# Down tile in two banks, dt by feature tile, and one chunk step's outputs behind a convolution's evacuation

## Chip, cores and metric

One core of a Trainium2 chip runs the whole kernel in one launch. The metric is the device time of that core in microseconds (us); the median of several runs is given. The engines are TensorE (PE, matmuls, with its weight loads shown as PEld), VectorE (DVE), ScalarE (ACT), GpSimd (POOL) and SyncE (SP), on whose queue the transfers (DMA) of this case are issued. Each engine works through its own instructions in order and waits on semaphores for the others.

## The reference, cut to what matters

One layer of a hybrid decoder: a half-step SwiGLU block, a mixer, a second half-step SwiGLU block, all with RMS norms, on 512 prompt tokens and 8 single-token samples (520 columns), width 1024, in float32.

```python
h = x
h = h + 0.5 * _swiglu(_rms_norm(h, ffn1_norm), w_gate1, w_up1, w_down1)   # FFN width 2816
m, p, c, s = _hybrid_mixer(_rms_norm(h, mix_norm), ...)
h = h + m
h = h + 0.5 * _swiglu(_rms_norm(h, ffn2_norm), w_gate2, w_up2, w_down2)
return _rms_norm(h, final_norm), ...

# the mixer
proj = h @ w_in                                  # u_pool | z | xbc | dt
pool_out = _pool_mix(u_pool, ...)                # window means of 2, 4, 8, 16 tokens, then a matmul per group
xbc = silu(causal_conv4(xbc));  dt = softplus(dt_raw + dt_bias)
# Mamba-2 SSD, per chunk of 128 tokens and group g of 8 heads (two groups):
Acs   = cumsum(dt * A)                           # within the chunk
y_diag = (C B^T * exp(Acs_l - Acs_s) * dt) x     # inside the chunk
y_off  = C h_prev * exp(Acs)                     # from the state of the chunk before
h_next = exp(Acs_last) * h_prev + B^T (exp(Acs_last - Acs) * dt * x)
y = rms_norm_per_group((y_diag + y_off + d_skip * x) * silu(z)) * ssd_norm
return cat(pool_out, y) @ w_out
```

## The kernel before, in words

Activations lie with the feature on the partition: `h` is 8 tiles of 128 x 520, and 520 columns are worked on in two `HALVES` of 260. A float32 product is made of three fp32r matmuls (`mm3`, lines 117, 120, 121): weights and activations are split in a high and a low part (`whi` by an ACT cast, line 107, `wlo` by a DVE subtraction, line 108; `xh` and `xl` likewise, lines 138 and 139).

The first SwiGLU block takes its 22 hidden tiles in chunks of 8, 8 and 6. At the end of a chunk, `down` makes the 8 output tiles `dn`, d = 0 to 7, each in a PSUM tile of two banks, one for each half (tag "BE", two such tiles; tag "A" is two tiles of one bank). One DVE instruction on 128 x 520 (`td`, line 369) scales a tile out of PSUM, and two adds (line 376) bring it into `h`. In the last chunk (`after` is set) each half then goes straight to the mixer's norm: `xh`, `xl`, a square on ACT (line 149) and a sum `acc` on DVE (line 150).

The mixer has a PSUM pool of 8 single banks, handed out in turn. It begins with the step size `dt`: 32 short matmuls (lines 639 to 642) into the two banks dt0 and dt1, one half after the other. Then come the input projections, convolutions and pooling, and the SSD work. The order of stages is written out by hand in `CONV_PLAN` and `GATE_PLAN`; letters name the stage: "x7" is the projection and convolution of x tile 7, "p3" the fourth pooling group, "c" and "m" its centring and mixing, "z" a z projection, "Aj" and "Bj" the two parts of chunk step j. Within and between stages a scheduler sets the order of instructions on each engine when the kernel is built; it weighs program order, dependences and its own cost model.

Chunk step j has chunk c = j % 4 and group g = j // 4, and its tiles carry both as two digits: step 1 is "10", step 2 "20", step 3 "30", step 4 "01". Part A (`ssd_a`): `pb` (a transpose and the scores), `px` (four transposes of X); a transfer `ab` (line 873) that spreads the cumulative sums of 8 heads over all partitions; `we` (line 877), 128 x 8 on POOL, then its exp; for c > 0 `E` and `cd`, exps of `ab` on ACT (lines 883, 885); the differences `ab` minus a per-token column, four by ACT (line 888) and four by DVE (line 890), and their exps (892, 893); `xdt` (line 895), DVE, which reads `px`; `xw` on POOL (line 898); `G`, the decay times the scores, in place in `ab` (line 899). Part B (`ssd_b`): matmuls `yo` (908), `pst` (911) and `yd` (914); the state `hst` (POOL 920, DVE 921); `E` times yo plus yd (924, 925); and four DVE instructions that add d_skip * X and write the output in X (line 928, "the outputs").

A projection's two banks are evacuated by `evac`, three DVE instructions (lines 622 to 624: half 0, the prompt part of half 1, the 8 samples) into `U` for a convolution or `PU` for a pooling group. Convolutions go on in `A` (ACT 708, DVE 710) and a SiLU into X (ACT 712, 713); pooling runs in doubling steps `PW` on POOL (line 742), then DVE (753) and casts. The order of DVE around the change, at 473 to 483 us of the profiled execution, was: hst10, the outputs of step 1, two ab30, U7's half 0, two ab30 and four ab01, U7's half 1 and samples, PW3, xdt30, E20, wlo_inz2. A wait for the convolution of x tile 7 is one for U7.

## Time and profile before

| what | value |
|---|---|
| median of 3 runs | 993.21 us (992.85 to 993.3) |
| the profiled execution | 992.8 us, its span 991.0 us |
| granted TensorE clock | 0.997 |
| busy: PE, DVE, ACT, POOL | 969.8, 800.0, 552.8, 87.4 us |
| chain that ended last | PE 90%, DVE 5%, POOL, DMA, ACT and issue 1% each |

The span runs from the first to the last instruction. Rows of instructions read: start in us, duration in us, engine, line, operation, output and inputs, shape, count, and in brackets the idle time before it with what ended it. Rows of waits read: engine, what waited, what it waited for, then total us, number of times, longest. A row of the windows gives the stretch, its length, the busy time and number of instructions of PE, PEld, DVE, ACT and POOL, then the granted clock, the DMA share and GB/s. One matmul is shown for 0.28 us though the next starts 0.12 us after it: they are pipelined.

### The profile page before, as it was taken

The page shows a single profiled execution, that of the slowest core. Times are in us where ns is not written, and L with a number is a line of the kernel's source. Part 1 is how long each engine was busy: PE and PEld are TensorE (multiplying, and loading weights), DVE is VectorE, ACT ScalarE, POOL GpSimd, SP SyncE. Part 2 cuts the span into 40 slices and gives each one's busy share as a digit, 9 for nine tenths or more (in the row PEclk, how much of TensorE's full clock was granted, in tenths as well). Part 3 has the DMA queues.
Part 4 walks back from the last instruction along what each step waited for, and adds up shares of the span by engine and source line. Part 5 has one row for each costly group of instructions (what it writes and reads, how often), then busy time and mean ns, then how long its engine had stood idle before and what let it go on. Part 6 is the DMA issues. An engine that isn't in the chain of part 4 may idle for free.

```text
span 991.0 us, 19414 instructions
## 1 busy us (share of the span) xinstructions
PE 969.8 (98%) x7852; PEld 951.0 (96%) x7852; DVE 800.0 (81%) x1295; ACT 552.8 (56%) x1011; POOL 87.4 (9%) x157
## 2 busy tenths in 40 slices
PE   7999999999999999999999999999999999999996
PEld 6899999999999999999899999899999999999995
DVE  7999656997569688788978997999967899668876
ACT  7566414664136455685668574666643566534653
POOL 0000000000000000156522000100013000120000
PEclk9999999999999999999999999999999999999998
DMA  6332322323222232262335232323246423363212
GB/s 188 121 128 95 120 86 86 128 86 129 85 86 81 91 126 85 82 206 100 124 114 186 81 125 86 113 98 128 100 117 198 162 88 127 120 181 119 96 65 87
DMA packets 42027, 114.48 MB, mean 116 GB/s; under 512 B 6408, under 2 KB 13512, under 8 KB 41936
## 3 DMA queue, kind: packets, MB, share of 16 engines
q1 hardware_dynamic: 38864, 103.78, 30.6%
q0 software_dynamic: 3072, 9.44, 3.7%
q8 instruction: 62, 1.02, 0.4%
q14 instruction: 29, 0.24, 0.1%
HBM read 105.86 MB, written 7.34 MB: 114 GB/s over the span
## 4 chain that ended last, share of the span: by engine, by line
PE 90%; DVE 5%; POOL 1%; DMA 1%; issue 1%; ACT 1%; SPq 0%; DVEq 0%; ACTq 0%
PE A L121 8%; PE A L117 8%; PE A L120 8%; PE dn L121 7%; PE dn L117 7%; PE dn L120 7%; PE BE L117 6%; PE BE L121 6%; PE BE L120 6%; PE wo L117 2%; PE wo L121 2%; PE wo L120 2%; PE P L234 2%; PE inz L117 2%; PE inz L121 2%; PE inz L120 2%
## 5 line engine op out<-in xcount | busy, mean ns | idle before, releaser
L117 PE MATMUL dn<-g,whi_1d 128*128 128x260 f32 x352 | 99.3, 283 | 0.2 <-DVE td L369 0.2
L120 PE MATMUL dn<-g,whi_1d 128*128 128x260 f32 x352 | 99.5, 283 | 0.0
L121 PE MATMUL dn<-g,wlo_1d 128*128 128x260 f32 x352 | 99.4, 283 | 0.0
L369 DVE SCALAR_TENSOR_TENSOR td<-dn,r_f 128x520 f32<-128x520 f32 x40 | 27.8, 698 | 72.7 <-PE dn L121 72.7
L121 PE MATMUL dn<-g,wlo_2d 128*128 128x260 f32 x256 | 72.5, 283 | 0.8 <-DVE wlo_2d L108 0.8
L117 PE MATMUL dn<-g,whi_2d 128*128 128x260 f32 x256 | 72.3, 282 | 0.0
L120 PE MATMUL dn<-g,whi_2d 128*128 128x260 f32 x256 | 72.3, 282 | 0.0
L117 PEld LDWEIGHTS dn<-g,whi_1d 128*128 128x128 f32 x352 | 66.1, 188 | 0.4 <-DVE td L369 0.4
L120 PEld LDWEIGHTS dn<-g,whi_1d 128*128 128x128 f32 x352 | 66.3, 188 | 0.0
L121 PEld LDWEIGHTS dn<-g,wlo_1d 128*128 128x128 f32 x352 | 66.2, 188 | 0.0
L299 ACT COPY ac<-A 128x260 f32<-128x260 f32 x123 | 45.6, 374 | 28.9 <-PE A L121 28.0
L107 ACT CAST whi_1d<-raw_1d 128x1024 fp32r<-128x1024 f32 (+1 forms) x24 | 23.5, 981 | 67.0 <-PE dn L120 54.2
L262 DVE TENSOR_TENSOR s<-raw 128x1024 f32<-128x1024 f32 x41 | 49.9, 1218 | 5.6 <-DMA raw<-in_w2gu 5.6
L234 PE MATMUL P<-xg_f,raw 128*128 128x260 f32 x192 | 45.4, 392 | 6.4 <-ACT sq_f L157 5.5
L121 PEld LDWEIGHTS dn<-g,wlo_2d 128*128 128x128 f32 x256 | 48.2, 188 | 1.0 <-DVE wlo_2d L108 1.0
L234 PEld LDWEIGHTS P<-xg_f,raw 128*128 128x128 f32 x192 | 36.9, 196 | 12.2 <-ACT sq_f L157 5.4
L117 PEld LDWEIGHTS dn<-g,whi_2d 128*128 128x128 f32 x256 | 48.3, 189 | 0.0
L120 PEld LDWEIGHTS dn<-g,whi_2d 128*128 128x128 f32 x256 | 48.2, 188 | 0.0
L117 PE MATMUL wo<-catg,whi_wo 128*128 128x260 f32 x128 | 37.2, 290 | 0.0
L117 PE MATMUL inz<-xh_mx,whi_inz 128*128 128x260 f32 x128 | 36.8, 287 | 0.1
L117 PE MATMUL inx<-xh_mx,whi_inx 128*128 128x260 f32 x128 | 36.4, 284 | 0.0
L121 PE MATMUL wo<-catg,wlo_wo 128*128 128x260 f32 x128 | 36.2, 283 | 0.0
(1341 smaller groups left out, 3936.7 us busy)
## 6 DMA issues: line engine op xcount, KB each, us to landing
raw<-in_w2gu SPq DMA_DIRECT2D x44, 512.0 KB, 4.5
raw<-in_w1gu SPq DMA_DIRECT2D x42, 512.0 KB, 4.5
raw_1d<-in_w1d SPq DMA_DIRECT2D x16, 512.0 KB, 4.5
raw_2d<-in_w2d SPq DMA_DIRECT2D x16, 512.0 KB, 4.4
raw_wo<-in_w_out SPq DMA_DIRECT2D x12, 512.0 KB, 4.9
ab<-scr_acs SPq DMA_DIRECT2D x8, 512.0 KB, 4.9
h<-in_state_ssm SPq DMA_DIRECT2D x16, 256.0 KB, 3.7
raw_inz<-in_w_in SPq DMA_DIRECT2D x8, 512.0 KB, 3.8
```

The costliest lines, as they stand in the source:

```text
L107: nc.scalar.copy(h, src)
L117: first = nc.tensor.matmul(ps, whi, xhi, start=start, stop=False, **kw)
L120: nc.tensor.matmul(ps, whi, xlo, start=False, stop=False, **kw)
L121: nc.tensor.matmul(ps, wlo, xhi, start=False, stop=stop, **kw)
L234: nc.tensor.matmul(self.banks[f, u][b][:, :HB], ws(self.raw[f][:, u], j + 4 * q), xg[:, slot[q]], start=j == q == 0, stop=j == 3 and q == ...
L262: nc.vector.tensor_tensor(out=s1, in0=diag, in1=up0, op=ALU.add)
L299: nc.scalar.copy(keep, out[:, :HB])
L369: nc.vector.scalar_tensor_tensor(out=t, in0=banks[d][:, :, :HB], scalar=-0.5, in1=self.nx[3].rearrange("p (b t) -> p b t", b=2), op0=ALU.mult,
```

## The change

Four edits, of which the third has two sides:

1. In the first block's last chunk, down tile 7 goes into two single banks (tag "A") instead of one two-bank tile, and each half is evacuated by itself (`done_by_half`: a 128 x 260 scale, an add, then the norm's preparation), at high priority.
2. dt's matmuls run over the feature tiles outside and the halves inside.
3. `we` moves from POOL to DVE, and `xdt` stands ahead of it in the program; `E` and `cd` get three buffers instead of two.
4. The four outputs of chunk step 1 are not issued in "B1" but by a stage "Y1" after "x7", and the scheduler may place them only behind the last evacuation instruction of that convolution (`held["evac"]`).

```diff
-    "b0 b1 d0 ... x6 c2 p3 A2 B1 x7 "
+    "b0 b1 d0 ... x6 c2 p3 A2 B1 x7 Y1 "
...
-                    banks[d] = ps[0].tile([P, 2, 512], F32, tag="BE", bufs=2, name=f"dn{self.i}_{d}_{c}")
+                    if after is not None and d == KD - 1:
+                        banks[d] = [ps[0].tile([P, 512], F32, tag="A", bufs=2, name=f"dn{self.i}_{d}_{c}{b}")
+                                    for b in range(2)]
+                    else:
+                        t = ps[0].tile([P, 2, 512], F32, tag="BE", bufs=2, name=f"dn{self.i}_{d}_{c}")
+                        banks[d] = t[:, 0], t[:, 1], t
...
+            def done_by_half(d):
+                for b, hs in enumerate(HALVES):
+                    t = self.wx.tile([P, 2, HB], F32, tag="tg", bufs=2, name=f"td{self.i}_{d}_{c}{b}")[:, b]
+                    nc.vector.scalar_tensor_tensor(out=t, in0=banks[d][b][:, :HB], scalar=-0.5, in1=self.nx[3][:, hs],
+                                                   op0=ALU.mult, op1=ALU.mult)
+                    nc.vector.tensor_tensor(out=h[:, d, hs], in0=t, in1=h[:, d, hs], op=ALU.add)
+                    after(d, b, hs)
...
-                done(d)
+                if after is not None and d == KD - 1:
+                    with tc.high_priority():
+                        done_by_half(d)
+                else:
+                    done(d)
...
-        nc.vector.tensor_tensor(out=buf[:, soff : ...], in0=bs[1][:, nb:HB],
+        held["evac"] = nc.vector.tensor_tensor(out=buf[:, soff : ...], in0=bs[1][:, nb:HB],
...
-    for b, hs in enumerate(HALVES):
-        for k in range(KD):
+    for k in range(KD):
+        for b, hs in enumerate(HALVES):
...
+        xdt = mp.tile([P, 8, 64], F32, tag="xdt", bufs=2, name=f"xdt{c}{g}")
+        nc.vector.tensor_tensor(out=xdt, ...)            # moved up from behind the exps
         we = mp.tile([P, 8], F32, tag="we", bufs=2, name=f"we{c}{g}")
-        nc.gpsimd.tensor_tensor(out=we, in0=ab[:, :, CH - 1], in1=atc, op=ALU.subtract)
+        nc.vector.tensor_tensor(out=we, in0=ab[:, :, CH - 1], in1=atc, op=ALU.subtract)
...
-            E = mp.tile([P, 4, P], F32, tag="E", bufs=2, name=f"E{c}{g}")
+            E = mp.tile([P, 4, P], F32, tag="E", bufs=3, name=f"E{c}{g}")
-            cd = mp.tile([P, 8], F32, tag="cd", bufs=2, name=f"cd{c}{g}")
+            cd = mp.tile([P, 8], F32, tag="cd", bufs=3, name=f"cd{c}{g}")
...
+        def out():
+            for q in range(4):
+                nc.vector.scalar_tensor_tensor(out=X[:, 4 * g + q, cs], ...)
+        if (c, g) == ssd(1):
+            held["out"] = out
+        else:
+            out()
+
+    def ssd_out(_):
+        with tc.issue_after(held["evac"]):
+            held.pop("out")()
```

How the built program moves: PE's order stays but for dt and two places of a few matmuls. ACT runs E30 and cd30 ahead of the SiLU of A5, with two more table loads, and we30 and the exponentials of ab30 ahead of the cast whi_inz0. SP issues out_nps ahead of the first half of raw_inz4, and ab01 behind both. DVE's order around x tile 7 becomes: E10, hst10, we01, three ab01, U7's half 0, one ab01, U7's half 1 and samples, the outputs of step 1, PW3, wlo_inz2, xdt30, E20; we30 and the four ab30 stand between U6's half 0 and half 1. In the first block, wlo_inbc0 stands ahead of tile 6's adds, and the halves of tile 7 between the xl and acc of tile 6.

More of the change, by code (lines that the diff above doesn't have):

```diff
@@ L39 @@
 CONV_PLAN = (
-    "b0 b1 d0 b2 b3 x0 x1 v0 d1 x2 x3 d2 X0 p0 y0 c0 A0 p1 x4 m0 x5 B0 c1 p2 m1 A1 x6 c2 p3 A2 B1 x7 "
+    "b0 b1 d0 b2 b3 x0 x1 v0 d1 x2 x3 d2 X0 p0 y0 c0 A0 p1 x4 m0 x5 B0 c1 p2 m1 A1 x6 c2 p3 A2 B1 x7 Y1 "
     "c3 X1 m2 A3 B2 e0"
@@ L363, in part @@
                         g = self.g[lo + k]
-                        mm3(banks[d][:, b, :HB], ws(wh, k), ws(wl, k), g[:, 0, b], g[:, 1, b], k == 0, k == n - 1)
+                        mm3(banks[d][b][:, :HB], ws(wh, k), ws(wl, k), g[:, 0, b], g[:, 1, b], k == 0, k == n - 1)
+            def done_by_half(d):
[5 more added lines that the diff above has]
+                    after(d, b, hs)
             def done(d):
@@ L368, in done @@
                 hd = h[:, d].rearrange("p (b t) -> p b t", b=2)
-                nc.vector.scalar_tensor_tensor(out=t, in0=banks[d][:, :, :HB], scalar=-0.5,
+                nc.vector.scalar_tensor_tensor(out=t, in0=banks[d][2][:, :, :HB], scalar=-0.5,
                                                in1=self.nx[3].rearrange("p (b t) -> p b t", b=2), op0=ALU.mult,
@@ L623, in evac @@
         nc.vector.tensor_tensor(out=buf[:, off + HB : off + SEQ], in0=bs[1][:, :nb], in1=r[:, HB:SEQ], op=ALU.mult)
-        nc.vector.tensor_tensor(out=buf[:, soff : soff + sstep * (NS - 1) + 1 : sstep], in0=bs[1][:, nb:HB],
-                                in1=r[:, SEQ:NT], op=ALU.mult)
+        held["evac"] = nc.vector.tensor_tensor(out=buf[:, soff : soff + sstep * (NS - 1) + 1 : sstep],
+                                               in0=bs[1][:, nb:HB], in1=r[:, SEQ:NT], op=ALU.mult).ins
     wdt = raw_tile("dt")[:, : KD * NH].rearrange("p (k h) -> p k h", k=KD)
@@ L875, in ssd_a @@
         atc = tok[:, 1, c, 8 * g : 8 * g + 8]
+        xdt = mp.tile([P, 8, 64], F32, tag="xdt", bufs=2, name=f"xdt{c}{g}")
+        nc.vector.tensor_tensor(out=xdt, in0=px.rearrange("p (a b) -> p a b", a=8),
+                                in1=dtc.unsqueeze(2).to_broadcast([P, 8, 64]), op=ALU.mult)
         we = mp.tile([P, 8], F32, tag="we", bufs=2, name=f"we{c}{g}")
-        nc.gpsimd.tensor_tensor(out=we, in0=ab[:, :, CH - 1], in1=atc, op=ALU.subtract)
+        nc.vector.tensor_tensor(out=we, in0=ab[:, :, CH - 1], in1=atc, op=ALU.subtract)
         nc.scalar.activation(out=we, in_=we, func=AF.Exp)
@@ L893, in ssd_a @@
         held["exp"] = nc.scalar.activation(out=G[:, ON_ACT:], in_=G[:, ON_ACT:], func=AF.Exp)
-        xdt = mp.tile([P, 8, 64], F32, tag="xdt", bufs=2, name=f"xdt{c}{g}")
-        nc.vector.tensor_tensor(out=xdt, in0=px.rearrange("p (a b) -> p a b", a=8),
-                                in1=dtc.unsqueeze(2).to_broadcast([P, 8, 64]), op=ALU.mult)
         xw = mp.tile([P, 8, 64], F32, tag="xw", bufs=2, name=f"xw{c}{g}")
@@ L926, in ssd_b @@
             yr = E
-        for q in range(4):
-            nc.vector.scalar_tensor_tensor(out=X[:, 4 * g + q, cs], in0=X[:, 4 * g + q, cs],
-                                           scalar=v("d_skip", 4 * g + q), in1=yr[:, q], op0=ALU.mult, op1=ALU.add)
+        def out():
+            for q in range(4):
+                nc.vector.scalar_tensor_tensor(out=X[:, 4 * g + q, cs], in0=X[:, 4 * g + q, cs],
+                                               scalar=v("d_skip", 4 * g + q), in1=yr[:, q], op0=ALU.mult, op1=ALU.add)
+        if (c, g) == ssd(1):
[5 more added lines that the diff above has]
+            held.pop("out")()
     zbox = []
@@ L1012, in mixer @@
         "B": lambda j: ssd_b(*ssd(j)),
+        "Y": ssd_out,
         "z": zproj,
```

## The prediction

> **What bounds the kernel now.** First the busy times of the page, then who TensorE (PE) waited for, then one table of windows to see where those waits lie.

> ```profile
> span 991.0 us, 19414 instructions
> ...
> PE 969.8 (98%) x7852; PEld 951.0 (96%) x7852; DVE 800.0 (81%) x1295; ACT 552.8 (56%) x1011; POOL 87.4 (9%) x157
> ```

> ```profile
> PE dt L640 <- DVE td L369: 0.9, 1, 0.9
> ...
> PE px L871 <- DVE xdt L895: 0.7, 1, 0.7
> ...
> PE pb L863 <- DVE U L624: 0.6, 1, 0.6
> PE yd L914 <- DVE U L622: 0.4, 1, 0.4
> ```

> ```profile
> 440.00:465.00 25.00, 25.00 (x212) 24.07 (x212) 22.31 (x41) 15.68 (x28) 16.44 (x28) 1.00 0.30 107
> ...
> 485.00:520.00 35.00, 35.00 (x293) 32.38 (x294) 28.72 (x60) 24.53 (x52) 7.04 (x7) 1.00 0.28 97
> ```

> PE is busy 98% of the span. The change adds and removes no matmul, so it can only act through PE's waits, and those it touches are four, each occurring once: 0.9 + 0.7 + 0.6 + 0.4 = 2.6 us. That is the ceiling of the gain, 0.26% of the span; a measurement of this kernel can tell about 0.2% (2.0 us) from no change. The first wait is at the step size (dt), at 367 us; the other three follow each other at 479 to 482 us. In the windows on both sides PE is busy all the time (25.00 of 25.00, 35.00 of 35.00), so what is won at 367 arrives at 478, and what is lost at 482 stays lost to the end.

> **Part 1: last down tile in two banks, dt by feature tile.**

> ```profile
> 361.88 1.05 ACT L107 CAST whi_inbc<-raw_dt 128x1024 fp32r<-128x1024 f32 x1 [0.64 <-PE dn L120]
> ...
> 363.63 1.22 DVE L108 TENSOR_TENSOR wlo_inbc<-raw_dt,whi_inbc 128x1024 fp32r<-128x1024 f32 x1
> 364.77 0.48 DVE L139 SCALAR_TENSOR_TENSOR xl_mx<-h,xh_mx 128x260 fp32r<-128x260 f32 x1
> ...
> 366.31 0.70 DVE L369 SCALAR_TENSOR_TENSOR td<-dn,r_f 128x520 f32<-128x520 f32 x1
> ...
> 368.41 0.76 DVE L376 TENSOR_TENSOR h<-td,h 128x260 f32<-128x260 f32 x2
> ...
> 365.99 0.28 PE L121 MATMUL dn<-g,wlo_1d 128*128 128x260 f32 x1
> 367.16 0.29 PE L640 MATMUL dt<-xh_mx,w 128*48 128x260 f32 x1 [0.88 <-DVE td L369]
> ...
> 367.40 0.28 PE L639 MATMUL dt<-xl_mx,w 128*16 128x260 f32 x1
> ```

> Matmuls of this size start 0.12 us apart; from the last down matmul (365.99) to the first of dt (367.16) are 1.17 us, so 1.05 are lost. dt0 lies in the bank that the last 128x520 evacuation (L369) was reading until 367.01. After the change dt0's bank belonged to tile 5 and is free; dt1's bank is the second half of tile 7, because the banks of the next pool are handed out in the same order as before. So the first feature tile's two dt0 matmuls can go at about 366.1, but the third, now dt1's first, waits for the second half's evacuation. With the halves in alternation that wait stands at the third matmul of dt; half by half it would stand at the seventeenth.

> When does this evacuation end? Walking VectorE (DVE): the cast whi_inbc ends at 362.93; wlo_inbc, now ahead of tile 6's adds, 1.14 (the step from its start to the next), to 364.2; two adds 0.7; the first half's evacuation 0.4 (estimate: an instruction on 128x260 takes 0.48 in the L139 row and starts its follower after 0.40), xl 0.4, one add 0.35, one acc 0.35: 366.4. The second half's evacuation ends at about 366.8, dt1 starts at 367.0. Before, the third dt matmul started at 367.40. Gain 0.4; bounds 0.2 (an evacuation queued 0.2 later) and 1.05 (the gap closed).

> **Part 2: exps of chunk step 3 run ahead.** Ahead of the place where the outputs move, three buffers for E and cd (names: two digits, chunk and group) free ScalarE (ACT) to run E30 and cd30 before X<-A5, where it used to run E30 at 476; and we30 and four ab30 subtractions (L890) stand on DVE in the middle of U6's evacuation.

> ```profile
> 446.97 0.33 SPq L873 DMA_DIRECT2D ab<-scr_acs  x1
> ...
> DMA to landing us min/median/max: 3.5/4.9/6.5
> ...
> 453.38 0.63 ACT L712 ACTIVATE X<-A 128x512 f32<-128x512 f32 x1 [2.45 <-DVE A L710]
> ...
> 460.01 1.05 ACT L107 CAST whi_inz<-raw_inz 128x1024 fp32r<-128x1024 f32 x1 [4.05 <-PE inx L120]
> 461.07 1.28 ACT L878 ACT_TABLE_LOAD   x1
> ...
> 455.09 1.23 DVE L108 TENSOR_TENSOR wlo_inx<-raw_inp,whi_inx 128x1024 fp32r<-128x1024 f32 x1 [1.34 <-ACT whi_inx L107]
> ...
> 463.77 0.79 DVE L710 SCALAR_TENSOR_TENSOR A<-U,h,A 128x544 f32<-128x544 f32 x1 [0.92 <-POOL PU L736]
> ...
> 467.41 0.68 DVE L895 TENSOR_TENSOR xdt<-px,tok 128x512 f32<-128x512 f32 x1
> 467.64 1.28 POOL L742 TENSOR_TENSOR PW<-PU 128x654 f32<-128x654 f32 x1
> ...
> 468.00 2.00 DVE L108 TENSOR_TENSOR wlo_inz<-raw_inz,whi_inz 128x1024 fp32r<-128x1024 f32 x1
> ```

> ACT was idle 2.45 before X<-A5. Into that go two table loads (exp, and silu again) of 1.28, two E of 0.64 (the row 476.42 below) and cd30 at 0.2: 4.0. That is 1.6 too much, 1.2 with the 0.4 from part 1. The wait for ab30 itself costs nothing: issued at 446.97 and landing by the median 4.9 later at 451.9, it is covered by the table load. DVE already waited 1.34 for the cast whi_inx behind X<-A5, so wlo_inx starts 1.2 later. Then we30 and four ab30 (about 1.0) come ahead of U6's second half, and on ACT the exponentials of ab30 (relus 1.3, exps 0.6, we30 0.2) ahead of whi_inz0: this cast starts at about 463.5 instead of 460.01, wlo_inz0 at 464.6 instead of 461.64. DVE's idle 0.92 at 463.77 takes some of it; xdt20 (467.41) comes at 469.4, 2.0 later. None of these is on PE's path yet: PE was full from 440 to 465 with these instructions queued, and nothing it reads before 478 comes within 2 us of xdt20. But wlo_inz1 behind xdt20 frees the buffer that raw_inz4 is loaded into.

> **Part 3: we on VectorE, and Y1.**

> ```profile
> 470.88 0.42 SPq L873 DMA_DIRECT2D ab<-scr_acs  x1
> ...
> 476.61 0.20 POOL L877 TENSOR_TENSOR we<-ab,tok 128x8 f32<-128x8 f32 x1 [0.90 <-DMA ab<-scr_acs]
> ...
> 449.68 1.12 DVE L928 SCALAR_TENSOR_TENSOR X<-X,h,yd 128x128 f32<-128x128 f32 x4
> ...
> 473.77 2.61 DVE L928 SCALAR_TENSOR_TENSOR X<-X,h,E 128x128 f32<-128x128 f32 x4
> ...
> 476.42 1.28 ACT L883 ACTIVATE E<-ab 64x512 f32<-64x512 f32 x2 [3.04 <-DVE X L928]
> ...
> 478.52 0.42 DVE L622 TENSOR_TENSOR U<-inx,r_mx 128x260 f32<-128x260 f32 x1
> 478.86 1.25 DVE L890 TENSOR_SCALAR ab<-ab,tok 128x128 f32<-128x128 f32 x6
> ...
> 480.43 0.75 DVE L753 SCALAR_TENSOR_TENSOR PW<-PW,PU 128x497 f32<-128x497 f32 x2
> 481.11 0.67 DVE L895 TENSOR_TENSOR xdt<-px,tok 128x512 f32<-128x512 f32 x1
> 481.44 1.04 POOL L920 TENSOR_TENSOR hst<-hst,cd 128x512 f32<-128x512 f32 x1
> ...
> 481.84 0.55 PE L871 MATMUL px<-ident,X 128*128 128x128 f32 x3 [0.66 <-DVE xdt L895]
> ...
> 482.31 1.26 DVE L108 TENSOR_TENSOR wlo_inz<-raw_inz,whi_inz 128x1024 fp32r<-128x1024 f32 x1
> ```

> `we` is eight instructions of 0.2 on GpSimd (POOL), an engine at 9%; on DVE they take as much, about 1.6 in all, hidden wherever DVE has slack. The exception is we01: it is the first reader of the transfer ab01, and in DVE's queue it stands **ahead** of U7's evacuation. Queued behind it: three ab01, U7 (L622, L623, L624), the four outputs of step 1, two PW3, wlo_inz2, xdt30. PE waits for U7 (yd20, pb01) and xdt30 (px01). POOL waited 0.90 for this same transfer, which cost PE nothing.

> When does ab01 land? Issued at 470.88, first read at 476.61: 5.7. On SP's queue stand ahead of it, after the change, out_nps and a raw_inz4 half. The first needs POOL's copy of the pooled state, which stands behind a pooling step (1.28, L742) and PU3's evacuation, itself late with xdt20; the second needs wlo_inz1, which starts at 470.0 and takes 1.2 alone or 2.0 beside a POOL instruction, as at 468.00. So both are ready at 471.2 to 472.0 and ab01 is issued at about 472.1. It lands at 475.6 with the shortest time of these transfers, at 477.0 with the median, at 477.8 with its own 5.7. I take 477.5, nearer to its own row, as the same transfers are around it. DVE gets to we01 between 474 and 475.8 (the outputs stood there at 473.77; at most 2.0 later) and waits.

> From there: we01 and four ab01 0.9 (0.2 apart, L890), U7 in three steps 0.8: 479.2, where before it was 480.4 (the start of L753, next in line). yd20 and pb01 no longer hold PE. Then the four outputs, 1.05 clean (1.12 measured) or 2.6 beside POOL. POOL's long pooling steps have ended by then, since nothing on DVE slows them while it idles; one hst step of 1.04 is likely to fall here or on wlo_inz2, and I put 0.6 for it. Two PW3 0.7, wlo_inz2 1.2 (**it was behind xdt30 and is now ahead of it**), xdt30 0.65: 479.2 + 1.05 + 0.6 + 0.7 + 1.2 + 0.65 = 483.4. px01 follows at 483.4 instead of 481.84: **1.6 us later**. The gains of 0.4, 0.4 and 0.6 ahead of it only lengthen this one wait, to 0.7 + 0.4 + 0.4 + 0.6 + 1.6 = 3.7 us. px01 heads the z projections, after which PE was full; the end moves by 1.6.

> On the contention: wlo_inz of 468.00 took 2.00 with a POOL instruction that had started at 467.64 and ended at 468.92; 0.8 over its usual 1.2, about what was left of that instruction. [...]

> **Sum.** The profiled execution took 992.8 us, 1.8 more than its span; 992.8 + 1.6 = 994.4. The median of the runs shown is 993.21, 0.4 more, and the forecast is made for that: 993.2 + 1.6 = **994.8 us**.

> **Rivals.**
> *Early transfer (not slower).* Everything in part 3 hangs on ab01. If it is issued where it was (470.9) and takes 3.5 to 4.5, or part 2's delay is smaller, it lands by 475.4. U7 is then done by 477, and the outputs, in part beside POOL's pooling steps (2.6), PW3 and wlo_inz2 end in time for xdt30 at about 481.3: px01 0.5 to 1.0 earlier, 992.4. Were all four waits gone, 990.6. The point from which it decides: landing about 475.8, 1.6 before my 477.5. For it speaks the 3.5 in the row; against it the own time of this transfer and the queue ahead of it. Chance 0.22, of which 0.10 beyond 0.2%.
> *Contended and late (slower by more).* ab01 lands 6.5 after its issue, at 478.6 (1.1 more), or outputs and wlo_inz2 both run beside POOL (0.9 and 0.8 instead of 0.6: 1.1 more); both: 2.2. 995.9 to 997.0. Chance 0.25.
> *Only the dt gain.* The later engines make up part 2 in idle time, we01 meets its data, and xdt30, behind one more 1.2 us instruction but clear of four ab30 (0.8) at that place, is where it was: px01 unmoved, the dt gain swallowed or kept, 992.8 to 993.2. It needs a landing at 475.8 to 476.2. Chance 0.08.
> *Forecast*, landing 476.5 to 478, between +0.6 and +2.6: chance 0.45.

> **How the numbers follow.** Of the forecast's 0.45 some 0.29 lie within 2.0 us of no change and 0.16 above; with 0.25 of the contended case that makes 0.41 slower. Faster is the far part of the early case, 0.10; within 0.2% the rest, 0.49. The range leaves out 0.1 at each end: 991.9, between the early case and the ceiling, and 997.0. The likeliest case alone: 993.8 to 995.8.

> **What would show it.** In PE's list of waits: dt behind the second half's evacuation, about 0.7 instead of 0.9; yd20 and pb01 gone; one wait of px for xdt of 3 to 4 us. On DVE: we01 idle 1.5 to 3.5 for the transfer ab; POOL's waits for ab gone. On ACT: two more table loads, X<-A5 about 1.2 later; ab01 issued at about 472. Wrong would be: no px wait over 1.5 us, a landing of ab01 by 475.8, or a new wait after 485.

## The result: 3.6 us slower, and the profile after

| | before | after |
|---|---|---|
| median | 993.03 us (6 runs, 991.83 to 993.32) | 996.60 us (6 runs, 996.09 to 997.83) |
| ratio | 1 | 1.0040, 95% from 1.0027 to 1.0053 |
| the profiled execution | 992.8 us | 996.29 us |
| granted TensorE clock | 0.997 | 0.994 |

The sign and the range of the forecast held (996.6 lies in 991.9 to 997.0); its size, +1.6, did not: the kernel lost 3.6 us by the medians and 996.29 - 992.8 = 3.5 us between the profiled executions. The page of after first: span, then each engine's busy time and instructions.

```profile
span 994.5 us, 19408 instructions
...
PE 972.0 (98%) x7852; PEld 953.2 (96%) x7852; DVE 797.2 (80%) x1304; ACT 555.1 (56%) x1013; POOL 82.6 (8%) x149
```

PE has as many matmuls as before and is busy 2.2 us longer. So waits alone cannot be the story: part of the loss is matmuls that took longer. PE's waits in after, of those that the change touches:

```profile
PE px L888 <- DVE xdt L894: 2.5, 1, 2.5
PE yd L931 <- DVE U L639: 2.1, 1, 2.1
...
PE dt L657 <- DVE td L374: 0.3, 1, 0.3
```

Before, px, pb and yd waited 0.7 + 0.6 + 0.4 = 1.7 here; now it is two waits, 4.6. At dt 0.9 became 0.3. Net, waits cost 2.9 - 0.6 = 2.3 us. The rest is in the windows of after. The column to read is the clock, third from the right:

```profile
480.00:482.00 2.00, 1.57 (x19) 1.21 (x19) 2.00 (x8) 2.00 (x5) 1.47 (x4) 0.87 0.06 9
482.00:484.00 2.00, 0.00 (x0) 0.00 (x0) 2.00 (x5) 2.00 (x6) 2.00 (x2) 0.50 0.67 229
484.00:486.00 2.00, 1.91 (x9) 1.82 (x10) 2.00 (x6) 1.10 (x4) 1.34 (x2) 0.50 0.31 107
486.00:488.00 2.00, 2.00 (x11) 2.00 (x11) 2.00 (x6) 1.05 (x3) 0.00 (x0) 0.50 0.00 0
488.00:490.00 2.00, 2.00 (x18) 2.00 (x18) 2.00 (x5) 0.80 (x4) 0.00 (x0) 0.92 0.00 0
```

The same 2 us of before (one row):

```profile
486.00:488.00 2.00, 2.00 (x19) 2.00 (x18) 2.00 (x6) 0.90 (x3) 0.39 (x1) 1.00 0.00 0
```

From 481.5 to 488.3 after's PE was granted half its clock, and a "full" 2 us counts 11 matmuls where before it counted 19. A busy share hides that: both rows say 2.00 of 2.00. PE's timeline in after shows the two gaps and the slow matmuls:

```profile
480.00 1.09 PE L931 MATMUL yd<-ab,xdt 128*64 128x128 f32 x16 [2.11 <-DVE U L639]
...
484.09 0.90 PE L888 MATMUL px<-ident,X 128*128 128x128 f32 x3 [2.52 <-DVE xdt L894]
...
486.15 0.42 PE L117 MATMUL inz<-xh_mx,whi_inz 128*128 128x260 f32 x1
486.37 0.42 PE L120 MATMUL inz<-xl_mx,whi_inz 128*128 128x260 f32 x1
...
492.12 1.05 PE L925 MATMUL yo<-BC,hst 128*128 128x128 f32 x8
```

And in before:

```profile
482.44 0.39 PE L117 MATMUL inz<-xh_mx,whi_inz 128*128 128x260 f32 x1
...
486.03 0.28 PE L121 MATMUL inz<-xh_mx,wlo_inz 128*128 128x260 f32 x1
486.15 0.28 PE L117 MATMUL inz<-xh_mx,whi_inz 128*128 128x260 f32 x1
...
488.30 0.94 PE L908 MATMUL yo<-BC,hst 128*128 128x128 f32 x7
```

Starts are 0.22 apart in after (486.15 to 486.37), 0.12 in before. px01 came at 484.09 instead of 481.84: 2.25 late. From px01 to the yo of step 3 the same matmuls took 8.03 us (484.09 to 492.12) instead of 6.46 (481.84 to 488.30): 1.57 more, about 16 z matmuls at 0.1 each. Together 3.82 at yo; a wait of the second block's down for wlo_2d, 0.8 before and 0.5 after, gives 0.3 back: 3.5.

Why the gaps: DVE's timeline in after, from the transfer to xdt30, and SP's.

```profile
478.55 0.34 DVE L897 TENSOR_TENSOR we<-ab,tok 128x8 f32<-128x8 f32 x1 [3.58 <-DMA ab<-scr_acs]
478.93 0.68 DVE L910 TENSOR_SCALAR ab<-ab,tok 128x128 f32<-128x128 f32 x3
479.52 0.42 DVE L639 TENSOR_TENSOR U<-inx,r_mx 128x260 f32<-128x260 f32 x1
...
480.45 1.13 DVE L947 SCALAR_TENSOR_TENSOR X<-X,h,E 128x128 f32<-128x128 f32 x4
481.50 0.80 DVE L770 SCALAR_TENSOR_TENSOR PW<-PW,PU 128x497 f32<-128x497 f32 x2
482.22 1.21 DVE L108 TENSOR_TENSOR wlo_inz<-raw_inz,whi_inz 128x1024 fp32r<-128x1024 f32 x1
483.36 0.68 DVE L894 TENSOR_TENSOR xdt<-px,tok 128x512 f32<-128x512 f32 x1
```

```profile
472.62 0.44 SPq L890 DMA_DIRECT2D ab<-scr_acs  x1
```

`we` of step 4 heads DVE's queue, and DVE stands idle for 3.58 us until ab01 is there, 5.9 after its issue. U7, on which yd20 waits, is queued behind it, and after U7 the outputs, PW3 and wlo_inz2 stand ahead of xdt30, on which px01 waits. So PE stops twice.

The transfer is not all that holds `we`. It takes 0.34 here and 0.15 alone (e6 below), and ends at 478.89, 0.01 after the last of three pooling steps on POOL. POOL in after:

```profile
477.34 1.54 POOL L759 TENSOR_TENSOR PW<-PW 128x640 f32<-128x640 f32 x1
```

### The profile page after: what moved, and what is told of

Its sections match the earlier page's. It is cut to its first block, busy times and chain, and to the rows that moved or that the text cites. A ratio compares the mean times of both kernels' runs of the same rounds, so it can differ in the third digit from the quotient of the medians.

```text
span 994.5 us, 19408 instructions
## 1 busy us (share of the span) xinstructions
PE 972.0 (98%) x7852; PEld 953.2 (96%) x7852; DVE 797.2 (80%) x1304; ACT 555.1 (56%) x1013; POOL 82.6 (8%) x149
## 4 chain that ended last, share of the span: by engine, by line
PE 93%; DVE 4%; DMA 2%; ACT 1%; issue 1%; SPq 0%; DVEq 0%; ACTq 0%
PE A L121 8%; PE A L117 8%; PE A L120 8%; PE dn L121 7%; PE dn L117 7%; PE dn L120 7%; PE BE L117 6%; PE BE L121 6%; PE BE L120 6%; PE P L234 5%; PE wo L117 2%; PE wo L121 2%; PE wo L120 2%; PE inz L117 2%; PE inz L120 2%; PE inz L121 2%
## 5 line engine op out<-in xcount | busy, mean ns | idle before, releaser
L120 PE MATMUL dn<-g,whi_1d 128*128 128x260 f32 x352 | 99.4, 283 | 0.0
L121 PE MATMUL dn<-g,wlo_1d 128*128 128x260 f32 x352 | 99.3, 282 | 0.0
L121 PE MATMUL dn<-g,wlo_2d 128*128 128x260 f32 x256 | 72.5, 283 | 0.5 <-DVE wlo_2d L108 0.5
L120 PE MATMUL dn<-g,whi_2d 128*128 128x260 f32 x256 | 72.3, 282 | 0.0
L120 PEld LDWEIGHTS dn<-g,whi_1d 128*128 128x128 f32 x352 | 66.3, 188 | 0.0
L121 PEld LDWEIGHTS dn<-g,wlo_1d 128*128 128x128 f32 x352 | 66.2, 188 | 0.0
L107 ACT CAST whi_1d<-raw_1d 128x1024 fp32r<-128x1024 f32 (+1 forms) x24 | 23.4, 980 | 67.0 <-PE dn L120 54.2
L121 PEld LDWEIGHTS dn<-g,wlo_2d 128*128 128x128 f32 x256 | 48.2, 188 | 0.7 <-DVE wlo_2d L108 0.7
L120 PEld LDWEIGHTS dn<-g,whi_2d 128*128 128x128 f32 x256 | 48.2, 188 | 0.0
L120 PE MATMUL inz<-xl_mx,whi_inz 128*128 128x260 f32 x128 | 36.8, 288 | 0.0
L121 PE MATMUL inz<-xh_mx,wlo_inz 128*128 128x260 f32 x128 | 36.8, 287 | 0.0
```

The lines of the kernel that those rows point to most:

```text
L107: nc.scalar.copy(h, src)
L120: nc.tensor.matmul(ps, whi, xlo, start=False, stop=False, **kw)
L121: nc.tensor.matmul(ps, wlo, xhi, start=False, stop=stop, **kw)
```

## The experiments

Each edit is shown against the kernel named. e1 to e12 were timed in five rounds beside the kernel before, whose median was 992.5 to 992.7 there, so ratios are the measure to compare by. "Issue" is when SP issued ab01, "clock" the stretch at 0.50 in the profile. A profile is of one execution and need not stand for all: that of e5 took 994.53, the longest of its twelve (from 990.87), that of e4 994.23 (from 991.93).

| run | median us | ratio to before, 95% | ab01 issue | px01 | clock 0.50 |
|---|---|---|---|---|---|
| after | 996.60 | 1.0040 [1.0027, 1.0053] | 472.62 | 484.09 | 481.5 to 488.3 |
| e1_part1 | 991.81 | 0.9991 [0.9982, 1.0000] | 469.83 | 480.49 | none |
| e2_fill | 999.23 | 1.0064 [1.0051, 1.0076] | 472.25 | 483.73 | 494.8 to 498.2 |
| e3_we01late | 993.36 | 1.0005 [0.9996, 1.0014] | 473.00 | 482.01 | 483.5 to 487.0 |
| e4_we01behindxdt30 | 993.28 | 1.0006 [0.9998, 1.0015] | 472.38 | 481.32 | 481.0 to 484.4 |
| e5_xdt30first | 992.29 | 0.9997 [0.9987, 1.0007] | 472.68 | 479.32 | 490.5 to 493.9 |
| e6_noY1 | 996.47 | 1.0035 [1.0021, 1.0048] | 472.40 | 483.40 | 480.5 to 487.4 |
| e7_we_gpsimd | 996.86 | 1.0035 [1.0022, 1.0048] | 471.46 | 482.06 | 481.7 to 488.6 |
| e8_Ebufs2 | 993.52 | 1.0008 [0.9998, 1.0018] | 469.63 | 480.18 | none |
| e9_E20first | 995.45 | 1.0031 [1.0019, 1.0043] | 469.19 | 479.75 | 491.1 to 494.5 |
| e10_part1_E3 | 993.22 | 1.0014 [1.0003, 1.0025] | 471.60 | 480.75 | none |
| e11_part1_weDVE | 992.21 | 0.9999 [0.9990, 1.0008] | 469.73 | 480.64 | none |
| e12_banks_only | 991.91 | 0.9993 [0.9984, 1.0002] | 469.96 | 481.13 | none |

**e1: the down tile and dt alone.** Edits 1 and 2 on the kernel before, nothing else.

```diff
 # against before
+                    if after is not None and d == KD - 1:
+                        banks[d] = [ps[0].tile([P, 512], F32, tag="A", bufs=2, ...) for b in range(2)]
...
-    for b, hs in enumerate(HALVES):
-        for k in range(KD):
+    for k in range(KD):
+        for b, hs in enumerate(HALVES):
```

> Part 1 alone: down tile 7 in two banks and dt by feature tile; we on GpSimd, E and cd in two buffers, no Y1, so the mixer is that of before. If the step-size gap is worth what the two traces show (dt's first matmuls 1.0 us earlier, its end and the first projection 0.6 us earlier) and TensorE keeps it, the time falls by 0.4 to 0.6 to about 992.5. Rival: the later waits at 478 to 482 us are set by other engines and swallow it: 993.0, no change.

Ratio 0.9991: about 0.9 us less where the theory had 0.4 to 0.6, with an interval that reaches 1.0000, so a gain is likely but not shown. There is no loss here, so it sits in edits 3 and 4. PE's waits in e1 are 0.7 at px01 for xdt30, 0.4 at pb01 for U7 and 0.3 at dt.

**e2: PE kept busy through the gaps.** In after, the pst matmul of step 2 runs three times and the score matmul of step 4 eleven times, each repeat writing the same values.

```diff
 # against after
+        for _ in range(11 if (c, g) == ssd(4) else 1):
             nc.tensor.matmul(pb[:, P : 2 * P], BC[:, g, cs], BC[:, 2 + g, cs], start=True, stop=True)
...
+        for _ in range(3 if (c, g) == ssd(2) else 1):
             nc.tensor.matmul(pst, bt, xw.rearrange("p a b -> p (a b)"), start=True, stop=True)
```

> The changed kernel with TensorE kept busy in its two idle stretches: two repeats of pst20 (1.9 us) ahead of yd20 and ten repeats of the score matmul (about 2.2 us) ahead of px01; both write again what they wrote. Theory: px01 is as late as in the changed kernel (484.1), but the granted clock stays at 1.00 where it fell to 0.50 up to 488.1, so sixteen z matmuls keep their 0.12 us steps: about 1.6 us less, 995.0. Rival: what goes beyond px01's delay of 2.25 us comes from the order of instructions behind px01, not from the clock: 996.6 as the changed kernel.

Both expectations missed the end time (999.23), yet the part that the run was made for came out. The window of the disputed stretch, first e2, then after:

```profile
478.00:490.00 12.00, 11.35 (x93) 9.68 (x92) 11.96 (x29) 7.24 (x18) 5.50 (x9) 1.00 0.16 58
```

```profile
478.00:490.00 12.00, 7.49 (x53) 7.03 (x54) 11.41 (x29) 8.03 (x22) 5.87 (x9) 0.72 0.18 61
```

With the gaps filled the clock stayed at 1.00, and from px01 to yo took 6.46 us as before, though DVE brought xdt30 only 0.4 earlier than in after. What spoiled the end is another thing: the scheduler moved px01's last transpose, which in after stands at 498.32, into the yd of step 3, where it waits for a SiLU. PE's timeline in e2:

```profile
490.19 1.05 PE L926 MATMUL yo<-BC,hst 128*128 128x128 f32 x8
...
494.20 0.33 PE L889 MATMUL px<-ident,X 128*128 128x128 f32 x1 [1.73 <-ACT X L729]
```

yo comes at 490.19, 1.93 earlier than after's 492.12, and then PE waits 1.73 and loses its clock from 494.8 to 498.2. The clock term of 1.57 is shown by the stretch to yo; the end time of this run says nothing on it.

This run also tells what holds `we`. DVE, then POOL, in e2:

```profile
477.14 1.38 DVE L898 TENSOR_TENSOR we<-ab,tok 128x8 f32<-128x8 f32 x1 [2.54 <-DMA ab<-scr_acs]
```

```profile
476.96 1.54 POOL L759 TENSOR_TENSOR PW<-PW 128x640 f32<-128x640 f32 x1
```

ab01 was there 1.41 earlier than in after, but `we` ended at 478.52, 0.02 behind POOL's step, and U7 gained only 0.37 (479.15 instead of 479.52), which is what POOL's step gained. The same holds in e8 and e9, where `we` takes 1.09 and 0.82 and ends 0.02 behind that step.

**e3 and e4: the first reader of ab01 behind U7, or behind xdt30.** Everything else as in after.

```diff
 # e3, against after
+        with tc.issue_after(held["evac"]) if (c, g) == ssd(4) else nullcontext():
             nc.vector.tensor_tensor(out=we, in0=ab[:, :, CH - 1], in1=atc, op=ALU.subtract)
```

```diff
 # e4, against after
+        behind = tc.issue_after(held["xdt"]) if (c, g) == ssd(4) else nullcontext()
+        held["xdt"] = nc.vector.tensor_tensor(out=xdt, ...).ins
...
+        with behind:
             nc.vector.tensor_tensor(out=we, in0=ab[:, :, CH - 1], in1=atc, op=ALU.subtract)
```

> The changed kernel with we01 alone held back behind U7's last evacuation, so VectorE evacuates U7 before it waits for the transfer ab01. Theory (the wait for ab01 at the head of VectorE's queue is the cause): U7 is out by 477, yd20 and pb01 do not wait, VectorE waits for ab01 behind the outputs until 478.5, xdt30 at 481 to 482, clock 1.00, 992.8 to 993.8. Rival (the outputs and wlo_inz2 ahead of xdt30 are the cause, wherever VectorE waits): 995.5 or more.

> The changed kernel with we01 held back behind xdt30. Theory: nothing on the way to px01 waits for ab01 any more; U7 out by 477, xdt30 by 480.5, px01 waits under 0.7, clock 1.00, and the gain of part 1 survives: 991.0 to 992.3. Rival: the late we01 and ab01 move the wait to step 4's own matmuls (yd01) or to the z projections through ScalarE, 993 or more.

e3 took back all but 0.5 us of the loss with ab01 as late as in after (473.00): the place of `we` ahead of U7 is one of two things that the loss hangs on (the other is the third buffer, e8 below). The clock was to stay at 1.00 and did not: yd20 and pb01 do not wait any more, but px01 waits 2.1, and from px01 to yo PE takes 8.00 (482.01 to 490.01), 1.54 more than in before. e4 was to gain more and did not. DVE in e4, and POOL in e4:

```profile
475.39 3.65 DVE L949 SCALAR_TENSOR_TENSOR X<-X,h,E 128x128 f32<-128x128 f32 x4
```

```profile
474.40 4.23 POOL L759 TENSOR_TENSOR PW<-PW 128x652 f32<-128x652 f32 x3
```

With U7 early, the outputs run beside POOL's pooling and take 3.65 instead of 1.13, and px01 still waits 2.1, in e3 and e4 for catp (L783), which stands just ahead of xdt30. POOL's three instructions took 4.23 in after too, where DVE was idle beside them: only DVE paid. In after the wait for ab01 (474.97 to 478.55) covered nearly all of this stretch (474.64 to 478.87).

**e5: xdt30 ahead of the outputs, of pooling's last part and of wlo_inz2, on top of e4.**

```diff
 # against e4
-    "... B1 x7 Y1 " "c3 X1 m2 A3 B2 e0"
+    "... B1 x7 " "X1 m2 A3 Y1 C3 B2 e0"       # C3: the centring, behind xdt30
...
     def ssd_out(_):
-        with tc.issue_after(held["evac"]):
+        with tc.issue_after(held["xdt"]):
             held.pop("out")()
...
+        if (c, g) == ssd(3):
+            later["inz2"] = held["xdt"]        # wlo_inz2 is issued behind xdt30
```

> Run 4 with xdt30 ahead of what stood before it: the outputs of step 1, the centring of pooling group 3 and wlo_inz2 are issued only behind xdt30, we01 as well. Theory: xdt30 follows px30 at about 476.7, so px01 follows pb01 without a wait at 479.3, no idle stretch over 1 us, clock 1.00, and against part 1 alone (991.8) the waits of 0.4 and 0.7 are gained too: 990.5 to 991.2. Rival: the outputs, three times as long beside GpSimd's pooling steps, and the late we01 push a later wait (X of A7, step 4's decay) onto TensorE: 992 or more.

px01 lost its wait altogether (479.32), and the time stayed at that of before (0.9997) instead of falling to 990.5 to 991.2. PE's only new wait in e5:

```profile
PE yd L939 <- DVE ab L924: 2.8, 1, 2.8
```

What DVE had put off was still to be done, and the decay product G of step 3 (ab, L924) was late instead. In the profiled execution the wait moved by 10 us and took its clock loss along.

**e6: without Y1; e7: `we` back on POOL; e8: two buffers of E and cd.** One part of the change undone in each.

```diff
 # e6, against after
-    "... A2 B1 x7 Y1 "
+    "... A2 B1 x7 "
 # e7, against after
-        nc.vector.tensor_tensor(out=we, in0=ab[:, :, CH - 1], in1=atc, op=ALU.subtract)
+        nc.gpsimd.tensor_tensor(out=we, in0=ab[:, :, CH - 1], in1=atc, op=ALU.subtract)
 # e8, against after
-            E = mp.tile([P, 4, P], F32, tag="E", bufs=3, name=f"E{c}{g}")
+            E = mp.tile([P, 4, P], F32, tag="E", bufs=2, name=f"E{c}{g}")
-            cd = mp.tile([P, 8], F32, tag="cd", bufs=3, name=f"cd{c}{g}")
+            cd = mp.tile([P, 8], F32, tag="cd", bufs=2, name=f"cd{c}{g}")
```

> The changed kernel without Y1: the outputs of step 1 stand ahead of we01 again. Theory (the wait for ab01 is the main cause, the place of the outputs worth about their own 1.1 us): they run while VectorE would wait, U7 is out at about 480.5 as in the changed kernel, xdt30 1.0 to 1.2 us earlier, px01 at 483, clock still 0.50 for a while: 995.0 to 995.8. Rival (Y1 is the main cause): 993.5 or less.

> The changed kernel with we back on GpSimd, all else kept. U7's half 0 now stands ahead of the first reader of ab01 on VectorE, its half 1 and samples behind four of them; xdt30 stands ahead of wlo_inz2. Theory: yd20 does not wait; pb01 waits for ab01's landing (478.5) plus 1.2, px01 for outputs, PW3 and xdt30 at about 482.3; TensorE is idle 1 and then 2 us, the clock falls once: 994.0 to 995.0. Rival (moving we is the whole cause): 993 or less.

> The changed kernel with E and cd in two buffers, so that ScalarE does not run E30 and cd30 early. Theory (that early run makes the chain up to xdt20 2 us late, and with it the issue of ab01): ab01 is issued at about 471 and lands by 476.7, U7 is out at 478.5, xdt30 at about 482, px01 0.2 to 0.8 later than in the kernel before: 993.5 to 994.5. Rival (the early E30 costs nothing): 996 or more.

e6: leaving the outputs in their old place makes no difference that these runs can tell (1.0035 beside 1.0040, with overlapping intervals); the 995.0 to 995.8 expected did not come. The outputs went back beside POOL and took 4.38, but within the time in which DVE had waited for ab01. DVE in e6:

```profile
474.68 4.38 DVE L947 SCALAR_TENSOR_TENSOR X<-X,h,E 128x128 f32<-128x128 f32 x4
478.98 0.15 DVE L897 TENSOR_TENSOR we<-ab,tok 128x8 f32<-128x8 f32 x1
```

Here no wait for ab01 is left on DVE at all, and the loss is about the same: the outputs beside POOL's pooling steps hold U7 as long as the transfer did.

e7: `we` on POOL does not help, because the next reader of ab01 on DVE, its four subtractions, takes over the place ahead of U7's second half. DVE in e7:

```profile
473.74 0.41 DVE L639 TENSOR_TENSOR U<-inx,r_mx 128x260 f32<-128x260 f32 x1
...
477.11 2.13 DVE L910 TENSOR_SCALAR ab<-ab,tok 128x128 f32<-128x128 f32 x4 [2.95 <-POOL we L897]
```

My theory had put a gain of some 2 us here; it was wrong on that, and the larger part of the reason is the clock. PE in e7:

```profile
482.06 0.90 PE L888 MATMUL px<-ident,X 128*128 128x128 f32 x3 [1.74 <-DVE xdt L894]
483.91 0.58 PE L117 MATMUL inz<-xh_mx,whi_inz 128*128 128x260 f32 x1 [0.95 <-DVE catp L783]
...
491.81 1.05 PE L925 MATMUL yo<-BC,hst 128*128 128x128 f32 x8
```

px01 is only 0.22 later than in before, and yo 3.51 later (491.81 to 488.30): 0.95 of that is the wait for catp, and 2.34 are slow matmuls.

e8 recovers 3.2 us (1.0040 to 1.0008). With two buffers E30 is not run ahead, SP issues ab01 at 469.63 instead of 472.62, and DVE waits for it ahead of U7 as in after, but earlier. DVE in e8, then PE:

```profile
475.02 1.09 DVE L897 TENSOR_TENSOR we<-ab,tok 128x8 f32<-128x8 f32 x1 [2.41 <-DMA ab<-scr_acs]
...
476.94 0.42 DVE L639 TENSOR_TENSOR U<-inx,r_mx 128x260 f32<-128x260 f32 x1
```

```profile
480.18 0.55 PE L888 MATMUL px<-ident,X 128*128 128x128 f32 x3 [0.61 <-DVE xdt L894]
...
482.23 0.39 PE L117 MATMUL inz<-xh_mx,whi_inz 128*128 128x260 f32 x1 [1.50 <-DVE E L941]
```

px01 was expected 0.2 to 0.8 later than in before and is 1.66 earlier; a wait of 1.5 for E20 follows, and the clock does not fall.

**e9: e8 with wlo_inz2 behind E20, to take that 1.5 away.**

```diff
 # against e8
+            yoE = nc.vector.tensor_tensor(out=E, in0=yo..., in1=E, op=ALU.mult)
+            if (c, g) == ssd(2): later["inz2"] = yoE.ins
...
+        with tc.issue_after(later[name]) if name in later else nullcontext():
             nc.vector.tensor_tensor(out=l, in0=src, in1=h.bitcast(F32), op=ALU.subtract)
```

> Run 8 (E and cd in two buffers) with wlo_inz2 issued behind E20 times yo20, the instruction that the first z matmul waited 1.5 us for. Theory: px01 at 480.2 as in run 8 and the z matmuls right behind it: 1.3 to 1.6 us off run 8, about 992.0, as good as part 1 alone (991.8). Rival: VectorE is full from 476 to 490 us, and whatever is moved back makes another wait of that size: 993 or more.

e9 was to gain 1.3 to 1.6 us on e8 and lost 2.3 by the ratios. As in e5 the wait went to the yd of step 3 and got longer there. PE's longest wait there, in e9:

```profile
PE yd L933 <- DVE ab L918: 2.4, 1, 2.4
```

In e5, e8 and e9 DVE is busy without a break from 478 to 490; taking one of its products earlier makes another late.

**e10 and e11: the third buffer, or `we` on DVE, each added to e1; e12: edit 1 without the new order of dt.**

```diff
 # e10, against e1
-            E = mp.tile(..., bufs=2, ...);  cd = mp.tile(..., bufs=2, ...)
+            E = mp.tile(..., bufs=3, ...);  cd = mp.tile(..., bufs=3, ...)
 # e11, against e1
-        nc.gpsimd.tensor_tensor(out=we, in0=ab[:, :, CH - 1], in1=atc, op=ALU.subtract)
+        nc.vector.tensor_tensor(out=we, in0=ab[:, :, CH - 1], in1=atc, op=ALU.subtract)
 # e12, against e1
-    for k in range(KD):
-        for b, hs in enumerate(HALVES):
+    for b, hs in enumerate(HALVES):
+        for k in range(KD):
```

> Part 1 alone (run 1) with E and cd in three buffers: the early E30 without we on VectorE and without Y1. Theory: xdt20 is 2 us later and ab01 lands at about 478; U7's half 1 stands behind ab01, so px01 comes about 1.5 us later than in run 1: 993.0 to 994.5. Rival (the early E30 hurts only where we01 heads VectorE's queue): within 0.5 of run 1, 991.8 to 992.3.

> Part 1 alone with we on VectorE, E and cd in two buffers, no Y1. Theory: ab01 lands at about 476 as in run 1, before VectorE is through with the outputs, so we01 waits little; but ab01 and ab30 stand ahead of U7's half 0, which costs yd20 up to 0.8: 991.8 to 992.8. Rival (moving we is harmful by itself): 994 or more.

> Part 1 without the new order of dt: the two single banks, and dt half by half. Theory: dt1's wait for the second half's evacuation moves behind sixteen matmuls of dt0 and vanishes, so dt loses 0.3 us less at its start; its last feature tile's xl comes no sooner, so the end is the same: the gap in front of dt under 0.1, the time within 0.3 of run 1. Rival: with half 0 first, its seventh feature tile is needed 1.9 us earlier than it is ready, and dt0 waits for it: 0.5 to 1.0 slower than run 1.

The third buffer alone delays ab01 to 471.60 and costs 1.4 us beside e1 by the medians (2.3 by the ratios, 1.0014 to 0.9991): PE's waits around px01 are 1.0 (for catp), 0.7, 0.6 and 0.4, in sum 2.7 in place of e1's 0.7 + 0.4, each short, so the clock stays up in the profile. The time came out as expected, but not by the way expected: ab01 was read at 476.58 and not at about 478, and px01 came 0.26 later than in e1, not 1.5. `we` alone leaves the issue at 469.73 and costs 0.8, within the intervals.

e10 and e7 have the same order on DVE from U7 on but for the outputs: ahead of U7 in e10, behind it in e7. px01 comes at 480.75 in e10 and at 482.06 in e7, and the ratios are 1.0014 and 1.0035. So with `we` on POOL the place of the outputs seems to matter, which it does not in e6. e12 is e1 within the measurement: two banks suffice, and half by half dt has no wait at all where by feature tile it has one of 0.3. e1 and e12 are the best versions found, some 0.7 to 0.9 us under before by the ratios; both intervals reach 1.0000 or beyond, so neither gain is shown.

## Why the forecast had the sign and not the size

- **Part 1** held. PE in after:

```profile
366.15 0.28 PE L659 MATMUL dt<-xl_mx,w 128*16 128x260 f32 x1
366.71 0.32 PE L657 MATMUL dt<-xh_mx,w 128*48 128x260 f32 x1 [0.28 <-DVE td L374]
```

  The third dt matmul waits for the second half's evacuation as forecast. It ended at 366.66, not 366.8; the wait fell by 0.6 (0.9 to 0.3), the gain put at 0.4.
- **Part 2** held: two more table loads, X<-A5 at 454.24 (0.9 late; 1.2 forecast), xdt20 at 469.08 (469.4 forecast). e8 and e10 show that this delay, which makes PE wait nowhere ahead of 478, is what ab01's issue hangs on: 469.2 to 470.0 in the runs with edit 1 and two buffers, 471.5 to 473.0 in those with three. It was forecast at 472.1 and came at 472.62. The traces show the link in SP's queue. SP's wait in after, and POOL's copy of the pooled state that ended it:

```profile
SPq L1026 <- POOL spool L766: 2.0, 1, 2.0
```

```profile
470.41 1.28 POOL L766 COPY spool<-PU 128x120 f32<-128x120 f32 x1
```

  The copy ends at 471.69, out_nps is issued at 471.72, raw_inz4's half at 472.23 and ab01 at 472.62. In before the copy had ended when out_nps came to its turn, and SP waited 1.8 for wlo_inz1 instead.
- **Part 3, landing.** "I take 477.5" was 1.05 short: `we` started at 478.55. Of that 0.5 is the later issue, the rest a transfer that took 5.9, near the 5.7 of its own row, where the working had mixed it with shorter ones. The rival "contended and late" had 478.6. (The rival "early transfer" puts 475.8 at 1.6 ahead of 477.5; it is 1.7.)
- **Part 3, contention.** POOL's long pooling steps had ended when the outputs ran, as forecast, though not because DVE stood idle beside them (4.23 here, and 4.23 beside the outputs in e4); but the last of them met `we`, which the working gave no time for: 0.2. The 0.6 put for the outputs or wlo_inz2 came out at nothing: 1.13 and 1.21. POOL's hst beside wlo_inz2 (482.24, 0.02 behind its start) paid instead, 2.10 where the one of 471.65 took 1.04. Landing, contention and smaller steps make px01 2.25 late instead of 1.6.
- **"yd20 and pb01 no longer hold PE"** was wrong for yd20. U7 was out 1.25 us later than the 479.2 reckoned (480.45), 1.05 by the landing and 0.2 by `we`, and PE had nothing ahead of it but yd20, ready at 477.9: two waits of 2.1 and 2.5 instead of one of 3.7. That PE has to stand somewhere until xdt30 makes no difference to px01's time.
- **The step that failed: "px01 heads the z projections, after which PE was full; the end moves by 1.6".** PE was full, but of matmuls 0.22 apart. The forecast priced a wait by its length alone; here a pair of waits of over 2 us had a second price, 1.57 us of slow matmuls behind them. It had no term for the clock at all. e2, e3 and e7 show that price apart: 0 without idle time, 1.54 behind one wait of 2.1, 2.34 in e7. In sum 1.6 forecast, + 0.65 for the later px01, + 1.57 for the clock, - 0.3 given back at wlo_2d: 3.5. The total fell within the rival "contended and late", 995.9 to 997.0, but only its landing came true; that the range held the result is luck, since no case in it has the clock. None of the three signs named for being wrong came either: the list watched waits and landings, not the clock.
- **The theory as it stands.** The loss goes when E and cd keep two buffers, so that E30 is not run early (e8), or when U7 stands ahead of every reader of ab01 on DVE (e3, e4): 3.2 to 3.5 us come back. Added to e1 one at a time, the third buffer costs 2.3 us by the ratios (e10) and `we` on DVE 0.8 (e11), edits 3 and 4 together 4.9; with intervals of about 1 us on each, whether the two make each other worse is not shown. By which way the early E30 does it stays open. It makes ab01 late (472.62 against 469.63 in e8) and POOL's pooling steps by nearly as much (the last ends at 478.88 against 476.09), and DVE is held by both: by the transfer to 478.55 and by POOL to 478.88 in after, by POOL alone in e6. No run was made to move one without the other; in e2, where the transfer happened to be there 1.41 sooner, U7 came only 0.37 sooner. The moved outputs cost nothing that can be told beside `we` on DVE (e6), but seem to beside `we` on POOL (e7, e10). The place of `xdt` ahead of `we` was not undone by itself.

## What to carry to other kernels

A transfer's first reader is a wait for everything behind it on its engine (3.58 us on DVE in after): put it behind what others need, above all when the change also delays the transfer. Look beside such a wait for what else would hold the engine if the data came sooner (in e2 the data came 1.41 sooner and U7 0.37). An added buffer is no free slack, since it lets work run ahead and push back what was due (ab01 by 1.77 us in e10 beside e1). When a change leaves TensorE idle for about half of 3.41 us or more, as ahead of the eight falls in the middle of these kernels (busy for 0.57 to 1.69), price the slower matmuls behind it too (1.57 us in after), and read the clock column beside the busy time, which was 2.00 of 2.00 us with 11 matmuls at 0.50 as with 19 at 1.00.

## What the runs showed of the hardware

Two stretches of one beat, first e2, then e8 (counted back from its fall at 983.50, at the end of the kernel, by 148 times 3.4133, an estimate); the columns are PE's busy time, the clock, the DMA share and GB/s:

```profile
491.41:494.83 3.42, 1.69 (x11) 1.00 0.00 0
494.83:498.24 3.41, 3.41 (x22) 0.50 0.02 5
```

```profile
478.33:481.74 3.41, 1.78 (x20) 1.00 0.39 144
481.74:485.15 3.41, 2.92 (x24) 1.00 0.14 59
```

The other surprise was what POOL does to a row of short DVE instructions: four outputs took 3.65 (e4) and 4.38 (e6) beside three pooling steps in a row and 1.13 in after, where the steps had ended, while POOL's own 4.23 did not change (4.23 in after and e4, 4.22 in e6).
